# Issuing a two-stream decoder layer in the order of its Python code, with the Strassen sums one half product earlier

## The chip, the core and the metric

The kernel runs on one core of a Trainium2 chip. A core has a matrix engine (TensorE, PE), a vector engine (VectorE, DVE), a scalar engine (ScalarE, ACT), GpSimd (POOL) and SyncE (SP), which here only sends DMA transfers. Each engine works off its own queue of instructions; semaphores make one engine wait for another. The metric is the device time of the whole kernel in microseconds (us).

## What is computed

One decoder layer on 256 tokens of width 2048 in float32: ten projections of `x`, causal attention, a chunked spatial gate, cross-attention into 256 memory tokens, three branch projections, merging by sigmoid gates, an output projection and a layer norm.

```python
proj = x @ w_in
q_a, k_a, v_a, z_a, u_g, v_g, z_g, q_c, z_c, g_logit = split(proj)
y_a = moba_attention(q_a, k_a, v_a) * silu(z_a)
y_g = spatial_gating(u_g, v_g, w_s, b_s, ln_v_g, ln_v_b) * silu(z_g)
y_c = memory_attention(q_c, mem @ w_mem_k, mem @ w_mem_v) * silu(z_c)
gates = sigmoid(g_logit)
merged = (gates[0] * (y_a @ w_branch_attn) + gates[1] * (y_g @ w_branch_sgu)
          + gates[2] * (y_c @ w_branch_mem))
x = layer_norm(DN_ALPHA * x + merged @ w_out)
```

## The kernel before

All products are made from split operands: `split` (L57 to L60) makes a rounded `hi` on ScalarE and the remainder `lo` on VectorE, and TensorE sums hi x hi, hi x lo and lo x hi. So each weight tile goes from a DMA through ScalarE and VectorE before TensorE can use it.

Two streams share the engines. The classic stream (`classic`) makes, in this order, the tiles of `zc`, `qc` with the memory attention, three tiles of `za`, the branch projection 2 (`gated_branch(2, 0)`), the rest of `za`, `q` and `k` with the causal attention, three tiles of `ug`, `gated_branch(0, 1)`, the rest of `ug`, the gating tiles `zg`, and `gated_branch(1, 2)`: 160 steps of half a weight chunk each. A chunk is 1 MB in a `raw` tile; `c_half` keeps two halves split ahead of the one in use, with three slots each for `hi` and `lo`. The Strassen stream (`s_stream`) makes eight blocks of 1024 columns (gate logits, `v`) by seven products of half blocks each: 112 steps. `s_prep(s + 2)`, called behind the matmuls of step s, makes the sum of weight blocks that a product needs (L311), splits it into `sh` and `sl` (four slots in all) and asks for the next block (`s_load`) once the old one has been read. The loop at the end of `classic` sets how the streams take turns: after classic step c it runs Strassen steps until their number has reached 112(c - 2)/144.

What a step leaves to do for others (evacuating accumulators, stores) is put on a list, `late`, and called behind the matmuls of the next step (`step`). Stages of the attention heads are called one by one by `tick`, at the end of each tile.

`gated_branch` (L697) takes each of four column blocks n with two accumulators, one for each half of the tokens, out of three slots `acc`. At the start of a block it loads the gate logits `sg` (L703) and takes their sigmoid (L704, ScalarE). After its four halves `gated` is put on `late`: it multiplies accumulator and gate (L726, VectorE), adds the sum so far `mp`, loaded at L725 (L728), and stores it, or in the last branch calls `merged` at once, in which TensorE transposes the result and the engines split it into `mhl`. Then come the output projection and `normalise`.

The order in which instructions stand in the queues is not that of the code: the context is opened with `schedule_with_timeline_sim=True`, so a planner with its own model of time orders them, by data dependences, free slots and priority. Three kinds of transfers are held in order by `tc.issue_after`. Before the streams start, `mem_values` and `mem_keys` project the memory tokens, while `x_stages` splits `x` and makes the four sums `F` that the Strassen products need (`sum_parts`, stores `xw` to `xf`). `s_load` of block B11 uses the two slots of `F`.

Of the kernel before, what the change touches and what calls it, by code (L numbers as in the profile page):

```python
# [11 lines left out]
ALU = mybir.AluOpType  # L12
# [15 lines left out]
def decoder_layer(ctx, tc, xT, memT, x_tok, w_st, w_mv, w_mk, w_zc, w_qc, w_za, w_qk, w_ug, w_zg,  # L28
                  w_br, w_o, w_sT, sgu_bc, ln_g, ln_b, out):
    nc = tc.nc  # L30

    const = ctx.enter_context(tc.tile_pool(name="const", bufs=1))
    big = ctx.enter_context(tc.tile_pool(name="big", bufs=1))
# [17 lines left out]
    def new_sps(name):  # L51
        return psum.tile([P, 512], F32, tag="sps", name=name, bufs=3)
# [5 lines left out]
    def split(hi, lo, v):  # L58
        nc.scalar.activation(hi, v, AF.Copy)  # L59
        nc.vector.tensor_tensor(lo, v, hi.bitcast(F32), op=ALU.subtract)  # L60
# [26 lines left out]
    ptr = {"load": 0, "half": 0}  # L87
    hold = {}

    loaded = {}  # L90
    riders = {}

    def load_chunk(i):

        if 0 < i < 16:
            with tc.issue_after(loaded[i - 1].ins):
                load_one(i)
        else:
            load_one(i)
        for fn in riders.pop(i, ()):  # L100
            with tc.issue_after(loaded[i].ins):
                fn()

    def load_one(i):
        if i % 3 == 2 and i < 16 or i >= OUT and (i - OUT) % 3 == 2:
            t = big.tile([P, 2, 1024], F32, tag="vg", name=f"raw{i}")
        else:
            t = wts.tile([P, 2, 1024], F32, tag="raw", name=f"raw{i}", bufs=2)
        raw[i] = t
        if i < 8:  # L110
            a = w2(f"mraw{i}", (P, 2, S))
            act_raw[i] = a
            if i == 0:

                for kk in range(2):
                    nc.sync.dma_start(a[:, kk], memT[:, kk])
                    for c in (slice(0, 512), slice(512, 1024)):
                        loaded[i] = nc.sync.dma_start(t[:, kk, c], chunks[i][:, kk, c])
                return
            nc.sync.dma_start(a, memT[:, 2 * i:2 * i + 2, :])  # L120
        for h in range(2) if i < 4 else (slice(0, 2),):
            loaded[i] = nc.sync.dma_start(t[:, h], chunks[i][:, h])
# [5 lines left out]
    def load_after(c):  # L128
        while ptr["load"] < len(chunks) and room_after(ptr["load"]) <= c:
            ptr["load"] += 1  # L130
            load_chunk(ptr["load"] - 1)
# [153 lines left out]
    UNITS = 8  # L285
    PRODUCTS = ("M1", "M5", "M6", "M3", "M7", "M4", "M2")
    FORM = {"M5": 1, "M6": 2, "M3": 4, "M7": 3}
    rt, shl, xsf, sp = {}, {}, {}, {}

    def s_load(u, blk, h):  # L290
        if u >= UNITS:
            return
        tag, bufs = ("rA", 2) if blk == 0 else ("rB", 4)
        t = wts.tile([P, 2048], F32, tag=tag, name=f"b{blk}_{u}_{h}", bufs=bufs)
        nc.sync.dma_start(t, w_st[u, blk, h])
        rt[u, blk, h] = t

    B11, B12, B22, B21 = range(4)

    def s_prep(s):  # L300
        u, r = divmod(s, 14)
        if u >= UNITS:
            return
        p, h = divmod(r, 2)
        p = PRODUCTS[p]
        if p in FORM:
            t = wts.tile([P, 4, 2 * P], F32R, tag="xsf", name=f"xf{s}", bufs=3)
            nc.sync.dma_start(t.bitcast(F32), xf_d[FORM[p], h])
            xsf[s] = t
        b = lambda blk: rt[u, blk, h]  # L310
        sub = lambda o, x, y: nc.vector.tensor_tensor(o, x, y, op=ALU.subtract)  # L311
        src = {"M1": B11, "M5": B11, "M6": B11, "M4": B11, "M3": B22, "M7": B12, "M2": B21}[p]
        if p == "M5":
            sub(b(B11), b(B12), b(B11))
        elif p == "M6":
            sub(b(B11), b(B22), b(B11))
        elif p == "M4":
            sub(b(B11), b(B21), b(B11))
        hi = wts.tile([P, 2048], F32R, tag="shl", name=f"sh{s}", bufs=4)
        lo = wts.tile([P, 2048], F32R, tag="shl", name=f"sl{s}", bufs=4)  # L320
        split(hi, lo, b(src))
        shl[s] = (hi, lo)
        if p == "M3":
            sub(b(B12), b(B22), b(B12))
            s_load(u, B21, h)
        elif p == "M7":
            s_load(u + 1, B12, h)
        elif p == "M4":
            s_load(u + 1, B11, h)
        elif p == "M2":  # L330
            s_load(u + 1, B22, h)

    def snap(name):
        return work.tile([P, 512], F32, tag="snap", name=name, bufs=5)

    def s_stream(finish):

        bank, kept = {}, {}

        def keep(name, ps):  # L340
            kept[name] = snap(name)
            nc.scalar.activation(kept[name], ps, AF.Copy)

        def result(u, t, n, ps, name):
            r = kept[name]
            nc.vector.tensor_tensor(r, ps, r, op=ALU.add)
            finish(u, t, n, r)

        def evacuate(u, p):
            if p == "M1":  # L350
                keep(f"k1_{u}", bank["b"])
            elif p == "M5":
                keep(f"k5_{u}", bank["d"])
            elif p == "M6":
                keep(f"k6_{u}", bank["b"])
            elif p == "M3":
                result(u, 0, 1, bank["d"], f"k6_{u}")
            elif p == "M7":
                keep(f"k7_{u}", bank["b"])
                result(u, 1, 1, bank["b"], f"k5_{u}")  # L360
            elif p == "M4":
                result(u, 1, 0, bank["c"], f"k7_{u}")
            else:
                result(u, 0, 0, bank["a"], f"k1_{u}")

        BANK = {"M1": "b", "M6": "b", "M7": "b", "M5": "d", "M3": "d", "M4": "c", "M2": "a"}
        for s in range(14 * UNITS):
            u, r = divmod(s, 14)
            p, h = divmod(r, 2)
            p = PRODUCTS[p]  # L370
            if h == 0 and p in ("M1", "M5", "M4", "M2"):
                bank[BANK[p]] = new_sps(f"s{p}_{u}")
            ps = bank[BANK[p]]
            hi, lo = shl.pop(s)
            for kk in range(4):
                k = 4 * h + kk
                if p in FORM:
                    ah, al = xsf[s][:, kk, 0:P], xsf[s][:, kk, P:2 * P]
                else:
                    k += 0 if p == "M1" else 8  # L380
                    t = P if p == "M4" else 0
                    ah, al = xhl[:, k, t:t + P], xhl[:, k, S + t:S + t + P]
                c = slice(kk * 512, (kk + 1) * 512)
                first = h == 0 and kk == 0 and p in ("M1", "M5", "M4", "M2")
                last = h == 1 and kk == 3
                nc.tensor.matmul(ps, ah, hi[:, c], start=first, stop=False, skip_group_check=True)  # L386
                nc.tensor.matmul(ps, ah, lo[:, c], start=False, stop=False, skip_group_check=True)  # L387
                nc.tensor.matmul(ps, al, hi[:, c], start=False, stop=last, skip_group_check=True)  # L388
            xsf.pop(s, None)
            s_prep(s + 2)  # L390
            if h == 1:
                late.append(lambda u=u, p=p: evacuate(u, p))
            yield
# [45 lines left out]
    def mem_keys():  # L439
        for j in range(8):  # L440
            def fin(ps, j=j):
                v = w1(f"mk{j}")
                joined(v, ps, f"mk{j}")
                store(mk_d[j], v)
            yield from channel_tile(mem_k, f"mk{j}", fin)

    def run(gen):

        left = [True]

        def go():
            left[0] = next(gen, "end") != "end"
        while left[0]:
            step(go)
            yield
# [4 lines left out]
    for i, _ in enumerate(run(mem_keys())):  # L460
        if x_work:
            x_work.pop(0)()
        if i in (2, 4):
            with tc.issue_after(loaded[ptr["load"] - 1].ins):
                s_load(0, B12, i // 2 - 1)
        if i in (10, 12):
            for blk in (B11, B22):
                with tc.issue_after(loaded[ptr["load"] - 1].ins):
                    s_load(0, blk, i // 2 - 5)
    while x_work:  # L470
        x_work.pop(0)()
        step(lambda: None)
    s_prep(0)
    s_prep(1)


    yhl = {}
# [297 lines left out]
    C_STEPS, S_STEPS = 160, 14 * UNITS  # L775
    LEAD, TAIL = 2, 14
    cs, ss = classic(), s_stream(s_finish)
    done_c = done_s = 0
    for _ in run(cs):
# [136 lines left out]
```

## Time and profile before

| | us |
|---|---|
| median of 3 runs | 1010.97 (1009.83 to 1012.68) |
| the profiled execution | 1014.38 |
| its span | 1012.7 |
| TensorE busy in it | 982.4 (97%) |
| VectorE busy in it | 820.6 (81%) |
| ScalarE busy in it | 590.6 (58%) |

The span goes from the first to the last instruction of the profile; the execution's own time is 1.7 us longer. A busy TensorE is not TensorE at its peak, since matmuls overlap; the step from the start of one to the start of the next is what it costs.

### The profile page before, as it was taken

The numbers are of one execution on the slowest core, as the hardware profiler recorded it, in microseconds if no ns is written. First come the engines' busy times: TensorE is split into PE (matmuls) and PEld (weight loads), VectorE is DVE, ScalarE is ACT, GpSimd is POOL, SyncE is SP. The second block draws the span as 40 slices with busy tenths as digits, with TensorE's granted clock in tenths as the row PEclk, the third lists the DMA queues.
The fourth block names the chain that finished last, engine by engine and source line by source line (L and its number), as shares of the span: only waits on it lengthen the run. The fifth ranks groups of instructions, "written<-read, shape, count | busy, mean of one in ns | idle before, by whom it ended". The sixth has DMA issues, their size and how long they took to land.

```text
span 1012.7 us, 12913 instructions
## 1 busy us (share of the span) xinstructions
PE 982.4 (97%) x4888; PEld 826.9 (82%) x4888; DVE 820.6 (81%) x800; ACT 590.6 (58%) x646; POOL 12.0 (1%) x17
## 2 busy tenths in 40 slices
PE   9999899999999999999999999979998999999995
PEld 7788788888888788888888888858877888878885
DVE  5865987898779799888979898899979877676657
ACT  5654665565577566556556566867555559554430
POOL 0000000000000000000000000000000010000000
PEclk9999999999999999999999999989999999999998
DMA  8899589738965897598379648937994785778622
GB/s 330 313 387 414 181 304 348 277 132 296 364 223 168 295 382 278 165 362 346 134 271 356 236 139 281 382 106 269 414 366 147 284 286 183 249 259 303 238 84 83
DMA packets 68126, 269.28 MB, mean 266 GB/s; under 512 B 7521, under 2 KB 21601, under 8 KB 45537
## 3 DMA queue, kind: packets, MB, share of 16 engines
q1 hardware_dynamic: 68064, 268.47, 72.2%
q8 instruction: 38, 0.62, 0.2%
q14 instruction: 24, 0.19, 0.0%
HBM read 245.37 MB, written 23.07 MB: 265 GB/s over the span
## 4 chain that ended last, share of the span: by engine, by line
PE 85%; DVE 5%; ACT 4%; DMA 3%; issue 2%; POOL 0%; SPq 0%; DVEq 0%; ACTq 0%
PE sM L386 9%; PE sM L387 9%; PE sM L388 9%; PE b L713 4%; PE b L714 3%; PE b L712 3%; PE zc L187 3%; PE k L187 3%; PE qc L187 3%; PE za L187 3%; PE q L187 3%; PE mk L187 3%; PE o L800 3%; PE o L799 3%; PE o L798 3%; PE mv L423 3%
## 5 line engine op out<-in xcount | busy, mean ns | idle before, releaser
L59 ACT ACTIVATE hi<-raw 128x1024 fp32r<-128x1024 f32 (+1 forms) x218 | 228.3, 1051 | 191.4 <-PE o L800 29.1
L60 DVE TENSOR_TENSOR lo<-raw,hi 128x1024 fp32r<-128x1024 f32 (+1 forms) x218 | 263.1, 1214 | 77.2 <-ACT hi L59 76.4
L60 DVE TENSOR_TENSOR sl<-b,sh 128x2048 fp32r<-128x2048 f32 x112 | 256.3, 2291 | 57.1 <-ACT sh L59 56.7
L59 ACT ACTIVATE sh<-b 128x2048 fp32r<-128x2048 f32 x112 | 214.4, 1915 | 99.6 <-PE sM L387 89.3
L311 DVE TENSOR_TENSOR b<-b,b 128x2048 f32<-128x2048 f32 x64 | 146.3, 2289 | 8.0 <-DMA b<-in_w_st_dram 7.8
L386 PE MATMUL sM<-sh,xf 128*128 128x512 f32 x256 | 101.3, 396 | 6.5 <-ACT sh L59 6.5
L387 PE MATMUL sM<-sl,xf 128*128 128x512 f32 x256 | 100.6, 393 | 2.5 <-DVE sl L60 2.5
L388 PE MATMUL sM<-sh,xf 128*128 128x512 f32 x256 | 100.2, 391 | 0.0
L387 PE MATMUL sM<-sl,xhl 128*128 128x512 f32 x192 | 76.8, 400 | 0.6 <-DVE sl L60 0.6
L386 PE MATMUL sM<-sh,xhl 128*128 128x512 f32 x192 | 77.4, 403 | 0.0
L713 PE MATMUL b<-lo,yhl 128*128 128x512 f32 x192 | 76.1, 397 | 1.2 <-DVE lo L60 1.2
L388 PE MATMUL sM<-sh,xhl 128*128 128x512 f32 x192 | 76.3, 397 | 0.0
L714 PE MATMUL b<-hi,yhl 128*128 128x512 f32 x192 | 74.9, 394 | 0.0
L712 PE MATMUL b<-hi,yhl 128*128 128x512 f32 x192 | 74.0, 398 | 0.9 <-ACT hi L59 0.9
L386 PEld LDWEIGHTS sM<-sh,xf 128*128 128x128 f32 x256 | 48.3, 189 | 18.3 <-ACT sh L59 7.9
L387 PEld LDWEIGHTS sM<-sl,xf 128*128 128x128 f32 x256 | 48.2, 188 | 12.9 <-DVE sl L60 3.2
L388 PEld LDWEIGHTS sM<-sh,xf 128*128 128x128 f32 x256 | 48.1, 188 | 10.3
L187 PE MATMUL ug<-xhl,hi 128*128 128x512 f32 x128 | 46.3, 400 | 1.5 <-ACT hi L59 1.5
L187 PE MATMUL q<-xhl,hi 128*128 128x512 f32 x128 | 46.5, 399 | 0.0
L187 PE MATMUL qc<-xhl,hi 128*128 128x512 f32 x128 | 46.2, 400 | 0.0
L187 PE MATMUL zc<-xhl,hi 128*128 128x512 f32 x128 | 45.7, 398 | 0.4 <-ACT hi L59 0.4
L187 PE MATMUL k<-xhl,hi 128*128 128x512 f32 x128 | 46.0, 397 | 0.0
(296 smaller groups left out, 1853.1 us busy)
## 6 DMA issues: line engine op xcount, KB each, us to landing
b<-in_w_st_dram SPq DMA_DIRECT2D x64, 1024.0 KB, 7.2
xf<-xf SPq DMA_DIRECT2D x64, 512.0 KB, 6.0
raw<-in_w_br_dram SPq DMA_DIRECT2D x24, 1024.0 KB, 6.8
raw<-in_w_qk_dram SPq DMA_DIRECT2D x16, 1024.0 KB, 7.3
raw<-in_w_o_dram SPq DMA_DIRECT2D x16, 1024.0 KB, 5.4
raw<-in_w_mk_dram SPq DMA_DIRECT2D x8, 1024.0 KB, 10.1
raw<-in_w_zc_dram SPq DMA_DIRECT2D x8, 1024.0 KB, 6.5
raw<-in_w_qc_dram SPq DMA_DIRECT2D x8, 1024.0 KB, 7.6
```

What stands on the lines that cost most here:

```text
L59: nc.scalar.activation(hi, v, AF.Copy)
L60: nc.vector.tensor_tensor(lo, v, hi.bitcast(F32), op=ALU.subtract)
L187: nc.tensor.matmul(ps, hi, x, start=first, stop=False)
L311: sub = lambda o, x, y: nc.vector.tensor_tensor(o, x, y, op=ALU.subtract)
L386: nc.tensor.matmul(ps, ah, hi[:, c], start=first, stop=False, skip_group_check=True)
L387: nc.tensor.matmul(ps, ah, lo[:, c], start=False, stop=False, skip_group_check=True)
L388: nc.tensor.matmul(ps, al, hi[:, c], start=False, stop=last, skip_group_check=True)
L423: nc.tensor.matmul(ps[t][n], lhs, rhs[:, n * 512:(n + 1) * 512], start=(k == 0 and rhs is hi and lhs is xh[t]), stop=(k == KT - 1 and lhs ...
L712: nc.tensor.matmul(ps[t], yh, hi[:, c], start=(k == 0), stop=False)
L713: nc.tensor.matmul(ps[t], yh, lo[:, c], start=False, stop=False)
L714: nc.tensor.matmul(ps[t], yl, hi[:, c], start=False, stop=(k == 7))
L798: nc.tensor.matmul(ps[:, 0:n], mh, hi, start=first, stop=False)
```

## The change

The context is put under a manual schedule: on every engine and on the DMA queue the instructions now stand in the order in which the Python code emits them. The `issue_after` blocks become plain calls. The sum of weight blocks is taken out of `s_prep` into `s_sum`, which is called with s + 3 just ahead of `s_prep(s + 2)`: it is emitted one half product ahead of the split that reads it. The subtraction for M3 stays behind its split.

```diff
+    ctx.enter_context(tc.manual_schedule())
...
         if 0 < i < 16:
-            with tc.issue_after(loaded[i - 1].ins):
+            if True:
                 load_one(i)
...
         for fn in riders.pop(i, ()):
-            with tc.issue_after(loaded[i].ins):
+            if True:
                 fn()
...
+    def s_sum(s):
+
+        u, r = divmod(s, 14)
+        if u >= UNITS:
+            return
+        p, h = divmod(r, 2)
+        other = {"M5": B12, "M6": B22, "M4": B21}.get(PRODUCTS[p])
+        if other is not None:
+            o = rt[u, B11, h]
+            nc.vector.tensor_tensor(o, rt[u, other, h], o, op=ALU.subtract)
+
...
-        if p == "M5":
-            sub(b(B11), b(B12), b(B11))
-        elif p == "M6":
-            sub(b(B11), b(B22), b(B11))
-        elif p == "M4":
-            sub(b(B11), b(B21), b(B11))
...
             xsf.pop(s, None)
+            s_sum(s + 3)
             s_prep(s + 2)
...
         if i in (2, 4):
-            with tc.issue_after(loaded[ptr["load"] - 1].ins):
+            if True:
                 s_load(0, B12, i // 2 - 1)
...
     s_prep(0)
     s_prep(1)
+    s_sum(2)
```

## Rows read from the trace of the kernel before

**Rows 1.** The page, busy us (share of the span) by engine, with instructions.

```profile
PE 982.4 (97%) x4888; PEld 826.9 (82%) x4888; DVE 820.6 (81%) x800; ACT 590.6 (58%) x646; POOL 12.0 (1%) x17
```

**Rows 2.** Waits of TensorE: waiter, what for, us in total, times, longest.

```profile
PE sM L386 <- ACT sh L59: 6.5, 3, 2.8
...
PE zc L187 <- ACT hi L59: 0.4, 1, 0.4
```

**Rows 3.** Timeline of TensorE: start, us, instruction, idle before and its releaser.

```profile
109.28 0.80 PE L386 MATMUL sM<-sh,xf 128*128 128x512 f32 x1 [2.84 <-ACT sh L59]
109.88 0.63 PE L387 MATMUL sM<-sl,xhl 128*128 128x512 f32 x1
110.31 0.63 PE L388 MATMUL sM<-sh,xhl 128*128 128x512 f32 x1
...
117.57 0.40 PE L187 MATMUL zc<-xhl,hi 128*128 128x512 f32 x1
117.80 0.28 PE L188 MATMUL zc<-xhl,lo 128*128 128x256 f32 x1
117.92 0.40 PE L187 MATMUL zc<-xhl,hi 128*128 128x512 f32 x1
...
679.19 0.79 PE L386 MATMUL sM<-sh,xf 128*128 128x512 f32 x1 [1.31 <-ACT sh L59]
```

**Rows 4.** Groups of VectorE by line and shape: busy us, mean ns, idle before.

```profile
L60 DVE TENSOR_TENSOR lo<-raw,hi 128x1024 fp32r<-128x1024 f32 x214 | 260.3, 1224 | 74.8 <-ACT hi L59 74.0
L60 DVE TENSOR_TENSOR sl<-b,sh 128x2048 fp32r<-128x2048 f32 x112 | 256.3, 2291 | 57.1 <-ACT sh L59 56.7
L311 DVE TENSOR_TENSOR b<-b,b 128x2048 f32<-128x2048 f32 x64 | 146.3, 2289 | 8.0 <-DMA b<-in_w_st_dram 7.8
...
L726 DVE TENSOR_TENSOR sg<-b,sg 128x512 f32<-128x512 f32 x24 | 15.6, 684 | 0.0
...
L663 DVE TENSOR_TENSOR vg<-vg,sc 128x256 f32<-128x256 f32 x16 | 6.4, 423 | 0.0
```

**Rows 5.** Groups of ScalarE by line and shape, the same columns.

```profile
L59 ACT ACTIVATE hi<-raw 128x1024 fp32r<-128x1024 f32 x214 | 225.8, 1059 | 189.0 <-PE o L800 29.1 <-PE b L714 25.1 <-PE zc L187 15.1
L59 ACT ACTIVATE sh<-b 128x2048 fp32r<-128x2048 f32 x112 | 214.4, 1915 | 99.6 <-PE sM L387 89.3 <-DVE b L311 4.8 <-DVE sg L726 3.5
...
L704 ACT ACTIVATE sg<-sg 128x512 f32<-128x512 f32 x24 | 14.9, 628 | 13.2 <-DMA sg<-gl 13.0
L704 ACT ACT_TABLE_LOAD x9 | 11.5, 1283 | 4.5 <-DMA sg<-gl 3.2 <-issue 0.9
```

**Rows 6.** Timelines of TensorE, VectorE and ScalarE in the first branch.

```profile
322.58 0.39 PE L712 MATMUL b<-hi,yhl 128*128 128x512 f32 x1
...
323.48 0.39 PE L387 MATMUL sM<-sl,xf 128*128 128x512 f32 x1
...
326.32 1.29 DVE L726 TENSOR_TENSOR sg<-b,sg 128x512 f32<-128x512 f32 x2
...
335.99 1.29 ACT L704 ACTIVATE sg<-sg 128x512 f32<-128x512 f32 x2 [4.39 <-DMA sg<-gl]
```

**Rows 7.** The transfers of line L703 (`sg`): time from issue to landing.

```profile
DMA to landing us min/median/max: 2.5/3.7/7.8
```

**Rows 8.** DMA issues by line: times, KB each, median us to landing.

```profile
b<-in_w_st_dram SPq DMA_DIRECT2D x64, 1024.0 KB, 7.2
...
xf<-xw SPq DMA_DIRECT2D x8, 512.0 KB, 7.4
```

**Rows 9.** Matmuls of L386 from 786 to 858: us, PE busy (count), PEld busy, clock.

```profile
786.00:858.00 72.00, 12.26 (x31) 5.88 (x32) 1.00 0.71 253
```

**Rows 10.** Timeline of VectorE in the last normalisation.

```profile
1002.86 2.86 DVE L815 SCALAR_TENSOR_TENSOR xres<-xres,fmv,g_bc 128x512 f32<-128x512 f32 x5
```

**Rows 11.** One stretch: us, busy us of PE, PEld, DVE, ACT, POOL, then clock.

```profile
655.00:742.00 87.00, 81.80 (x346) 66.03 (x345) 79.44 (x71) 53.38 (x50) 0.00 (x0) 0.94 0.73 282
```

More of the change, by code (lines that the diff above doesn't have):

```diff
@@ L467, in decoder_layer @@
             for blk in (B11, B22):
-                with tc.issue_after(loaded[ptr["load"] - 1].ins):
+                if True:
                     s_load(0, blk, i // 2 - 5)
```

## The prediction

> **What bounds the kernel now.** The page's busy table comes first. The reader is to see TensorE at 97% and VectorE at 81% [rows 1]: TensorE sets the time, so the change can only bring what TensorE waits, and can cost whatever new waits it makes. Second, TensorE's own waits: six kinds of them, from 6.5 down to 0.4 us (the first and the last are shown [rows 2]), are waits for a split half (`hi`, `lo`, `sh`, `sl`) that came in an unlucky order, 13.6 us in all. Third, the timeline of TensorE behind such a wait: after 2.84 us without work the matmuls of 512 columns start 0.43 us apart, the lower of its two clock levels, where 0.23 is the step at the upper one [rows 3]. Three such stretches stand in the trace (6, 7 and 13 matmuls at 0.2 us extra each; the first and the last are shown), 5.4 us. So all that a perfect order could give back is 13.6 + 5.4 = 19 us; the start, the last reductions and the output lie outside both streams.
>
> **Base.** The profiled execution took 1014.4 us (span 1012.7 us), 3.4 us above the median of the runs. Sums are made on 1014.4; 3.4 comes off at the end.
>
> **What the edit does, part by part.** The `issue_after` blocks go; inside a strict order they say nothing, cost 0. `s_sum` moves a subtraction of 2.29 us [rows 4] ahead of the split that reads it by one half: it fills the 1.92 us in which ScalarE makes `sh` [rows 5], and `sl` behind it comes 0.4 us later. There are 64 before and after; cost 0, since that split is wanted two halves later (above 10 us). The strict order is the real change: each queue now runs the Python order, and a wait holds all that is behind it. In the even parts (the tiles of `zc`, `qc`, `za`, `q`, `k`, `ug`) this fits: `late` puts every evacuation one step after its matmuls, and splits are emitted two halves ahead. TensorE's steps are 2.79 us for a classic half (8 pairs of 0.35 [rows 3]) and 2.72 us for a Strassen half or a branch half (12 x 0.227); VectorE needs 1.22 for a classic half and 2.29 + 2.29 x 64/112 = 3.6 for a Strassen half [rows 4]. So there the 19 us come back: **-19**.
>
> **Gated branches, second accumulator.** `gated_branch` takes two accumulators per column block n from a ring of three. The fourth matmul of block n+1 (0.68 us into its first half) therefore needs the multiply L726 that frees an accumulator of block n, and that multiply is emitted one step late. Now the planner fills the gap: from 322.58 on it runs a few matmuls of the first token tile and eleven Strassen matmuls until the multiply has come at 326.32 [rows 6]. In strict order TensorE stands. Call T the start of block n+1's first half.
> Counting by the loop's rule (Strassen halves done after classic step c: 112(c-2)/144 rounded up), blocks start at steps 39, 43, 47, 51; 103, 107, 111, 115; 145, 149, 153, 157. The first of each branch needs no multiply. In four of the others (43, 47, 51, 115) a Strassen half ends just at T. Its slots come free at T, ScalarE makes the next `sh` (1.92), VectorE `sl` (2.29), and only then the multiply (0.69) [rows 4, 5]: T + 5.0. Stall 5.0 - 0.7 = 4.3, **4 x 4.3 = 17**.
> In the other five the step before is a classic one, so L726 is emitted behind the first half's own split. ScalarE has ahead of that split the two sigmoids of block n+1, whose operand is sent for at about T (behind the weight load that waits for the split before). With the median landing of 3.7 us [rows 7]: operands T + 3.75, two sigmoids of 0.63 T + 5.0, `hi` 1.06 T + 6.1, `lo` 1.22 T + 7.3, multiply T + 8.0 [rows 4, 5]. Stall 7.3. Four times (111, 149, 153, 157) 29. At 107 SyncE is held until about T + 3.3 by a Strassen load that waits for the reading of its slot, so 10.6. One table load, 1.3 [rows 5], in the last branch. **Together 41.** Lower end with the shortest landing, 2.5: 35; upper with 7.8: 62 [rows 7]. In the last branch `merged` puts TensorE's transposes right behind the adds; the last add ends at T + 10, as does the rest of the stalled half, so they cost only at the end of the stream, where nothing is between: an operand `mp` of the same size, 3.7, then an add, a multiply and an add: **5** (4 to 9).
> The Trainium skill, "DMA: Bandwidth & Descriptors", section "Anatomy of one DMA", gives about 2.0 us plus the bytes over 436 GB/s for one transfer, 2.6 us for 256 KB (an estimate from that fit, which is for another issuing path). The shortest landing agrees with it, the median of 3.7 does not [rows 7]. By the page's price the 41 would be some 35. The row decides, since a 1 MB weight load is in flight ahead of it each time.
>
> **First block of the middle branch** (step 103): SyncE held to T + 4.6, landing T + 8.3, table load and sigmoids T + 10.9, split T + 13.2, wanted at T + 10.9: **2** (0 to 6).
>
> **From memory keys to classic.** `s_load(0, B11, 1)` takes the slot of the second `F` tile, which the last `sum_parts` frees; that one waits for an earlier store (7.4 us [rows 8]). So it is sent for at the end of the memory keys and lands 7.2 us later [rows 8]; `sh` of half 1 stands ahead of the classic `hi` on ScalarE, and `sl` and the sum ahead of `lo` on VectorE: about 14.3 us after the keys' end, wanted at 5.6: **9** (2 to 12).
>
> **The gating tiles** (`zg`). Now only 31 of the first matmuls of Strassen steps lie there, some 8 halves [rows 9]; strictly it is 12.4. VectorE then has 16 x 1.22 + 12.4 x 2.29 + 8 sums of 2.29 + gating (L663, 6.4 [rows 4], and five groups of 8 x 0.42, as long as one of L663) + four evacuations of 0.69, 92 us beside some 82 of TensorE (16 x 2.79 + 12.4 x 2.72 and the mixes); the two halves of lead hold about 5: **5** (0 to 10). POOL's few masks keep their order, 0.
>
> **Ends.** At the start ScalarE takes the second `memhl` piece ahead of the first `hi`: 1. In the last normalisation the five L815 now stand behind the square root instead of beside it [rows 10]: 0.5. **1.5** (0.5 to 3).
>
> **Clock.** After 1.3 to 2.8 us of idling 6 to 13 matmuls ran on the lower level [rows 3], 1.2 to 2.6 us lost, 1.9 in the middle. Eleven stalls above 2.5 us: **21** (13 to 36).
>
> **Sum:** 17 + 41 + 5 + 2 + 9 + 5 + 1.5 + 21 = 101.5, less 19: +82.5, 1096.9; less 3.4: **1094 us**. With all lower ends (17 + 35 + 4 + 0 + 2 + 0 + 0.5 + 13 - 19 = 53) 1064, with all upper ones and only 13 given back (18 + 62 + 9 + 6 + 12 + 10 + 3 + 36 - 13 = 143) 1154.
>
> **Rivals.**
> (a) Short stalls. If the sigmoids' operands come in time (SyncE runs further ahead than I think), only the chains within engines are left: 4 x 4.3, and 5 x (1.06 + 1.22 + 0.69 - 0.68 = 2.3), 3 at the end, 4 elsewhere, 36 in all, and 5 for the clock: 36 + 5 - 19 = +22, less the 3.4 **1033 us**. For: the landing's minimum of 2.5 [rows 7]. Against: such operands already keep ScalarE waiting 4.39 us at 336 [rows 6].
> (b) Faster. The multiply is done before the fourth matmul asks: that needs L726 ahead of the split of the same step on VectorE, so that it ends by T + 0.7. It decides all nine stalls and their clock. Then 19 us come back and only 1.5 to 4 are paid: **995 us**. For: none of TensorE's waits now names L726. Against: it is emitted behind the split, and a strict queue can't put it ahead.
> (c) VectorE becomes the bound. Each chain that goes from VectorE to ScalarE and back (softmax, gated values) idles VectorE 0.5 to 1.5 us, some 24 times, in parts where it is as much as 91% busy (79.44 of 87 us [rows 11]): up to 30 us on top, **1124 us**, inside the forecast's upper half.
> (d) The order isn't strict, slots being given out by the planner: then little changes, **1008 to 1014**.
> The Trainium skill, "PSUM — Partial Sum Buffer", section "Engine vs sequencer instructions", says that the queues of ScalarE and VectorE are strictly first in, first out, and that matmuls start and end in program order. By that rule (b) would need another emission. The trace of before can't show it, its program order being the planner's.
>
> **How the numbers follow.** Forecast with (c): 0.66. (a) 0.16. (b) 0.13. (d) 0.03, of it 0.02 within the resolution. Beyond 1154: 0.02. About 0.3% is what a measurement of this kernel can tell from no change. The range leaves out (b), (d) and the top: 1018 to 1140; the likeliest case's own is 1064 to 1154. Faster 0.13, same 0.02, slower 0.85.
>
> **What the changed profile would show.** Right: TensorE waits for L726 nine times, 4 to 11 us each; ScalarE L704 waits on the load `sg`; the granted clock is below 1 in the slices of the three branches and 1 in the tiles between them; the stall of 660 to 680 is gone; VectorE's busy sum stays near 820. Wrong: no such waits (then (a) or (b)); a TensorE idle spread evenly over all stages (then (c)). The sum fails first in the landing of `sg` and in the clock's price, as they carry 62 of the 101.5 us.

## The result, and the profile after

The changed kernel takes 1169.1 us (1166.97 to 1172.03 in four runs) where the kernel before takes 1010.6: a ratio of 1.157, 95% interval 1.1535 to 1.1599. The forecast was 1094, in a range of 1018 to 1140: the direction and the place were right, the size was too small by 75 us. The measured time lies beyond even the sum of all the forecast's upper ends, 1154, to which it gave a chance of 0.02. The new lines stand eight lower in the code at the branches: L726 is now L734, L728 is L736, L703 is L711, L704 is L712, L712 to L714 are L720 to L722, L59 and L60 are L60 and L61.

The page of the changed kernel, busy us (share of the span) by engine, then the granted clock of TensorE in forty slices:

```profile
PE 1018.8 (87%) x4888; PEld 845.7 (72%) x4888; DVE 831.7 (71%) x800; ACT 568.8 (49%) x638; POOL 9.5 (1%) x17
...
PEclk9999999999988899999999997879899999778998
```

Against [rows 1] the span grew by 153.8 us (1166.5 less 1012.7). TensorE's busy time grew by 36.4 with the same 4888 instructions: that is, in the main, the lower clock. The other 117.4 are idle time. VectorE and ScalarE do about the work that they did before (831.7 us for 820.6, 568.8 for 590.6).

TensorE's waits in the changed kernel (waiter, releaser: us in total, times, longest), where [rows 2] began with 6.5 us:

```profile
PE b L720 <- DVE sg L734: 72.6, 9, 15.8
PE ug L189 <- DVE lo L61: 12.0, 3, 8.5
PE b L720 <- ACT hi L60: 7.5, 4, 3.3
PE zc L188 <- ACT hi L60: 6.9, 2, 6.2
PE mT L748 <- DVE sg L736: 6.3, 2, 6.1
PE b L721 <- DVE lo L61: 5.1, 7, 0.8
PE zg L189 <- DVE lo L61: 4.7, 3, 3.2
PE sM L392 <- DMA xf<-xf: 4.3, 6, 1.1
PE sM L393 <- DVE sl L61: 4.1, 3, 2.6
```

The first row is the forecast's row: nine waits for the multiply that frees an accumulator. Four of these nine, in the timeline of TensorE (start, us, instruction, idle before and its releaser): two behind a Strassen half, two behind a classic step, and behind one of them the step of the matmuls:

```profile
353.04 0.79 PE L720 MATMUL b<-hi,yhl 128*128 128x512 f32 x1 [4.11 <-DVE sg L734]
...
795.21 0.79 PE L720 MATMUL b<-hi,yhl 128*128 128x512 f32 x1 [4.02 <-DVE sg L734]
...
733.52 0.79 PE L720 MATMUL b<-hi,yhl 128*128 128x512 f32 x1 [15.85 <-DVE sg L734]
734.12 0.63 PE L721 MATMUL b<-lo,yhl 128*128 128x512 f32 x1
734.54 0.63 PE L722 MATMUL b<-hi,yhl 128*128 128x512 f32 x1
734.97 0.63 PE L720 MATMUL b<-hi,yhl 128*128 128x512 f32 x1
...
996.80 0.79 PE L720 MATMUL b<-hi,yhl 128*128 128x512 f32 x1 [9.59 <-DVE sg L734]
```

Why the longest is so long is read from the other three queues between 712 and 736 us. First the DMA queue, then ScalarE, then VectorE:

```profile
714.80 6.85 SPq L296 DMA_DIRECT2D b<-in_w_st_dram  x2
722.46 0.33 SPq L123 DMA_DIRECT2D raw<-in_w_br_dram  x1
722.84 0.97 SPq L711 DMA_DIRECT2D sg<-gl  x2
723.90 0.92 SPq L733 DMA_DIRECT2D mp<-mc  x2
...
716.54 0.63 ACT L761 ACTIVATE vg<-k 128x512 f32<-128x512 f32 x1 [3.25 <-DVE k L352]
...
729.40 1.27 ACT L712 ACTIVATE sg<-sg 128x512 f32<-128x512 f32 x2 [9.48 <-DMA sg<-gl]
730.57 1.04 ACT L60 ACTIVATE hi<-raw 128x1024 fp32r<-128x1024 f32 x1
...
719.01 2.29 DVE L61 TENSOR_TENSOR sl<-b,sh 128x2048 fp32r<-128x2048 f32 x1 [2.50 <-ACT sh L60]
...
731.64 1.23 DVE L61 TENSOR_TENSOR lo<-raw,hi 128x1024 fp32r<-128x1024 f32 x1 [9.21 <-ACT hi L60]
732.79 0.68 DVE L734 TENSOR_TENSOR sg<-b,sg 128x512 f32<-128x512 f32 x1
```

It reads as a chain. The block begins at 717.0 (733.52 less the 15.85 and three matmuls of 0.23). Before that ScalarE has stood 3.25 us at the evacuation `vg<-k`, and VectorE 2.50 us for the `sh` behind it, so that `sl`, the last reader of a Strassen block's slot, ends at 721.3. The DMA queue is held by two Strassen blocks until 721.7 and sends the gates `sg` at 722.84; they land at 729.4; ScalarE has stood 9.48 us at the sigmoid, with the split `hi` behind it; VectorE has stood 9.21 us at `lo`, with the ready multiply behind it; TensorE stands for the accumulator. Three engines wait for one 256 KB load that none of the waiting instructions but the sigmoid needs. Not all of the 15.85 us is the load's: in two runs below in which `sg` is not waited for, or hardly at this block, it still stalls 6.5 and 6.6 us by the chain that begins at `vg<-k`.

### The profile page after: what moved, and what is told of

Same layout as the page of the kernel before. It is cut to its first block, busy times and chain, and to the rows that moved or that the text cites. A ratio compares the mean times of both kernels' runs of the same rounds, so it can differ in the third digit from the quotient of the medians.

```text
span 1166.5 us, 12791 instructions
## 1 busy us (share of the span) xinstructions
PE 1018.8 (87%) x4888; PEld 845.7 (72%) x4888; DVE 831.7 (71%) x800; ACT 568.8 (49%) x638; POOL 9.5 (1%) x17
## 4 chain that ended last, share of the span: by engine, by line
PE 49%; DVE 18%; DMA 17%; issue 8%; ACT 7%; SPq 1%; ACTq 0%; DVEq 0%
DVE sl L61 6%; PE sM L392 5%; DMA sg<-gl 5%; PE sM L393 5%; DVE lo L61 5%; PE sM L394 5%; PE mv L430 3%; DMA xf<-xf 3%; PE o L807 3%; PE o L806 3%; ACT sh L60 3%; PE o L808 3%; ACT hi L60 3%; DVE b L310 2%; PE b L720 2%
## 5 line engine op out<-in xcount | busy, mean ns | idle before, releaser
L61 DVE TENSOR_TENSOR lo<-raw,hi 128x1024 fp32r<-128x1024 f32 (+1 forms) x218 | 262.6, 1212 | 179.8 <-ACT hi L60 178.4
L61 DVE TENSOR_TENSOR sl<-b,sh 128x2048 fp32r<-128x2048 f32 x112 | 256.4, 2289 | 64.3 <-ACT sh L60 60.4
L60 ACT ACTIVATE sh<-b 128x2048 fp32r<-128x2048 f32 x112 | 214.2, 1912 | 151.6 <-PE sM L393 145.1
L60 ACT ACTIVATE hi<-raw 128x1024 fp32r<-128x1024 f32 (+1 forms) x218 | 225.6, 1042 | 91.1 <-PE o L808 28.8
L720 PE MATMUL b<-hi,yhl 128*128 128x512 f32 x192 | 85.6, 446 | 80.2 <-DVE sg L734 72.6
L310 DVE TENSOR_TENSOR b<-b,b 128x2048 f32<-128x2048 f32 x48 | 109.6, 2284 | 0.0
L720 PEld LDWEIGHTS b<-hi,yhl 128*128 128x128 f32 x192 | 40.8, 213 | 94.7 <-DVE sg L734 76.4
L721 PE MATMUL b<-lo,yhl 128*128 128x512 f32 x192 | 83.6, 436 | 5.1 <-DVE lo L61 5.1
L722 PE MATMUL b<-hi,yhl 128*128 128x512 f32 x192 | 82.2, 428 | 0.0
L394 PEld LDWEIGHTS sM<-sh,xf 128*128 128x128 f32 x256 | 48.5, 189 | 11.1
L712 ACT ACTIVATE sg<-sg 128x512 f32<-128x512 f32 x24 | 15.0, 630 | 82.1 <-DMA sg<-gl 81.9
L721 PEld LDWEIGHTS b<-lo,yhl 128*128 128x128 f32 x192 | 41.1, 214 | 16.0 <-DVE lo L61 7.7
L188 PE MATMUL zg<-xhl,hi 128*128 128x512 f32 x128 | 48.9, 418 | 1.5 <-ACT hi L60 1.5
```

Source lines behind the costliest of these rows:

```text
L188: nc.tensor.matmul(ps, hi, x, start=first, stop=False)
L310: nc.vector.tensor_tensor(o, rt[u, other, h], o, op=ALU.subtract)
L720: nc.tensor.matmul(ps[t], yh, hi[:, c], start=(k == 0), stop=False)
L721: nc.tensor.matmul(ps[t], yh, lo[:, c], start=False, stop=False)
L722: nc.tensor.matmul(ps[t], yl, hi[:, c], start=False, stop=(k == 7))
```

## The experiments

The kernel before took 1011 to 1012 us beside each of these runs. The theories that the expectations name: A, a strict queue holds the multiply behind a split and behind the sigmoids' loads, and the clock falls after each stall. B, the order costs a little everywhere, VectorE being the bound. C, TensorE's own fixed order is the cause. D, the late landing of loads behind a held DMA queue is the cause by itself. E, the loss is a product of late loads and of queues that stand at them; F, the engines' fixed orders suffice without the loads.

**1. Which half of the change costs.** The sums moved, the planner's order kept:

```diff
-        if p == "M5":
-            sub(b(B11), b(B12), b(B11))
...
+            s_sum(s + 3)
             s_prep(s + 2)
```

> The planner's order of the kernel before, with only the sums of weight blocks issued one half product earlier (the other half of the change alone). Theory A: the sums have no part in the loss, 1011 us, within 3 us of the kernel before. Rival: the sums take VectorE's slots and the loss is partly theirs: 1020 us or more.

Measured: 1011.5 us, ratio 0.9998 (0.9988 to 1.0008). The moved sums cost and bring nothing; the whole loss is the order's.

**2. Which engine's order costs.** The same kernel with the strict order on some queues only:

```diff
-    ctx.enter_context(tc.manual_schedule())
+    ctx.enter_context(tc.manual_schedule(engines={...}))
```

> Strict order on the DMA queue alone. Theory A: the queue's order matters only where an engine is held at a load, 1011 to 1025 us. Rival D (the late landing of loads behind a held DMA queue is the cause by itself): 1050 us or more.

> Strict order on ScalarE and VectorE alone; TensorE and the DMA queue as the planner orders them. Theory A: these two queues carry most of it, 1040 to 1100 us. Theory C and rival D: 1025 us or less.

> Strict order on TensorE alone; the planner orders the other engines and the DMA queue. Theory A: the multiply and the splits can be put ahead of what waits, so the nine stalls are short: 1015 to 1035 us. Theory C: most of the loss is here, 1100 us or more.

> Strict order on ScalarE, VectorE, GpSimd and the DMA queue; TensorE's matmuls are ordered by the planner. Theory A (queues of ScalarE and VectorE hold what TensorE needs, so TensorE has little else to run in a stall): about half of the loss stays, 1060 us or more. Theory C (TensorE's own fixed order makes the loss, because it can no longer run the other stream's matmuls while one operand is late): 1030 us or less.

> Strict order on TensorE, ScalarE, VectorE and GpSimd; only the DMA queue as the planner orders it. Theory E (a product: the loads sg, mp and the weights are sent late by a strict DMA queue, and ScalarE and VectorE stand at them with all that is behind): most of the branches' loss goes, 1080 us or less, and the waits of ScalarE for sg fall from 82 us to under 20. Theory F (TensorE's, ScalarE's and VectorE's fixed orders suffice; the accumulators are late whatever the loads do): 1130 us or more.

| strict order on | us | over before |
|---|---|---|
| the DMA queue | 1032.5 | 21 |
| ScalarE and VectorE | 1059.0 | 48 |
| TensorE | 1046.1 | 35 |
| all but the DMA queue | 1100.4 | 88 |
| all but TensorE | 1146.5 | 135 |
| all | 1169.1 | 158 |

The intervals of the ratios are at most 0.6% to either side. One caution: these kernels have the change's plain calls in place of `issue_after`, so where the DMA queue isn't strict nothing holds the first loads in order. The stage ahead of `zc` loses 18 to 22 us in the four kernels of this study of which that holds (the second, third and fourth line, and one of experiment 3), and 8 to 12 in the others; some 10 us of these lines belong to it.

TensorE's own order adds 23 us to the rest (158 less 135). The DMA queue's adds 70 (158 less 88, and some 10 more by the caution), but by itself only 21: what the queues cost does not add up, one order's cost depends on the others'. The rows of the loads `sg` say how: who waited for them (us, times), and their time from issue to landing. First with all strict, then with the DMA queue alone, then with all but the DMA queue:

```profile
  ACT sg L712: 81.9, 14
...
DMA to landing us min/median/max: 5.0/6.0/9.6
```

```profile
  ACT sg L712: 14.7, 5
...
DMA to landing us min/median/max: 5.0/6.0/9.1
```

```profile
  ACT sg L712: 0.8, 2
...
DMA to landing us min/median/max: 2.5/4.8/8.9
```

A strict DMA queue makes the landing long whoever orders the rest. By itself that cost only 5 us of stage loss in the branches (worked out as in experiment 3), since ScalarE was given other work before the load; it costs much in a ScalarE that must stand at it. So D alone falls short (1032.5 is above A's 1025 and far below D's 1050), and E, which expected 1080 or less for the last kernel where F expected 1130, is nearer to its 1100, though its bound was missed too: the nine waits remain there, with 41.3 us instead of 72.6:

```profile
PE b L720 <- DVE sg L734: 41.3, 9, 8.1
```

C falls with the kernel in which the planner orders TensorE alone: the accumulator is no longer named in its waits, and the time is lost all the same, at the splits behind the sigmoids:

```profile
PE b L720 <- ACT hi L60: 44.8, 18, 7.6
PE sM L392 <- DMA xf<-xf: 26.8, 15, 4.1
```

TensorE strict alone came out above A's 1035 for another reason, a wait of its transposes in the causal attention (21.7 us in four). The planner, which fixes TensorE's order by its own model before the run, found little else to put there while the other engines stand; no run here lets TensorE choose as it goes.

**3. Which stages cost.** The strict order switched off for the three branches, and the reverse, at the classic steps where they begin and end:

```diff
+        if done_c in (38, 102, 144):
+            strict.close()
+        elif done_c in (55, 119):
+            strict.enter_context(tc.manual_schedule())
```

> Strict order everywhere except in the three gated branches (classic steps 38 to 54, 102 to 118, 144 to the end of the streams), which the planner orders. By the prediction's sum the parts outside the branches cost 9 + 5 + 1.5 and some clock and give back most of 19: 1008 to 1020 us. By the losses per stage of the changed kernel's trace (time of a stage less its matmuls at full clock, after less before) these parts cost about 45 us: 1050 us.

> Strict order only in the three gated branches; the planner orders the rest. By the prediction's sum 17 + 41 + 5 + 2 + about 18 of clock, less 5 given back: 1011 + 78 = about 1090 us. By the losses per stage of the changed kernel's trace the branches cost 105 us: 1116 us. If the loss needs a queue that is strict from the start on, under 1050 us.

Measured: 1041.3 us without the branches, 1125.4 with the branches alone; 29 and 113 over before, 142 of the 158 together. Both came out nearer to the losses by stage (1050 and 1116) than to the prediction's sum (1008 to 1020 and 1090), and strict branches alone suffice: their loss does not need a queue that is strict from the start. To see where, each stage's loss was worked out from the timelines of TensorE: the stage's length less its matmuls at the upper clock (0.227 us for 512 columns, in proportion for fewer, 0.061 for 128). Stages end where the next tile's first matmul starts, but branch 1 ends behind its own last matmul, so that the wait for its last add stands under the output, which ends with its last matmul; a few matmul records are missing, so a figure is good to about 2 us.

| loss, us | to `zc` | `zc`, `qc` | `za` (both) | branch 2 | `q`, `k` | `ug` (both) | branch 0 | `zg` | branch 1 | output |
|---|---|---|---|---|---|---|---|---|---|---|
| before | 9.3 | 11.4 | 5.5 | 1.6 | 8.2 | 7.4 | 12.6 | 5.6 | 2.6 | 2.1 |
| all strict | 12.2 | 23.3 | 4.3 | 35.6 | 13.7 | 17.4 | 47.3 | 15.1 | 39.2 | 11.1 |
| strict but in the branches | 10.6 | 25.1 | 4.6 | 4.3 | 12.6 | 8.1 | 7.9 | 13.4 | 1.5 | 2.4 |
| strict in the branches | 21.0 | 6.8 | 5.4 | 27.2 | 8.3 | 20.5 | 39.8 | 7.7 | 34.9 | 1.9 |

All strict, the branches lose 105 us more than before (122.1 less 16.8) and the rest 48. Strict in the branches alone they lose 85 more; the run's other 22 over before stand mainly ahead of `zc` (11.7), where nothing holds the first loads in order, and in `ug` (13.1), on both sides of a strict branch.

**4. What in the branches holds the multiply.** First, the multiply one step earlier:

```diff
                 if half == 3:
+                    for t in range(2):
+                        nc.vector.tensor_tensor(g[t], ps[t], g[t], op=ALU.mult)
                     late.append(lambda n=n, ps=ps, g=g: gated(b, order, n, ps, g))
```

> Strict order as in the changed kernel; only the multiply that frees an accumulator is issued right behind the fourth half of its block instead of one step later. Theory A (the loss sits where a strict queue holds that multiply behind a split and behind the sigmoids' loads, and the clock falls after each such stall): the nine waits for L734 (72.6 us) shrink to under 1 us each; in the five blocks that follow a classic step the weight half behind the sigmoids is still late by 3 to 5 us each, so some 20 us come back as waits for hi and lo; the clock gives back some 20: 1169 - 73 + 20 - 20 = about 1096 us. Theory B (strict order costs a little in every stage, VectorE being the bound): the time moves elsewhere and stays above 1140 us.

Measured 1153.3 us in one run: a miss by 57. The waits for the multiply did shrink, and were given back at the next instruction behind the same load; TensorE's waits in this kernel (waiter, releaser: us, times, longest):

```profile
PE mT L749 <- DVE sg L737: 27.0, 4, 7.5
PE b L720 <- ACT hi L60: 22.0, 7, 6.6
PE b L720 <- DVE sg L725: 15.8, 5, 5.4
```

Second, the gates early (`fetch` sends the two loads `sg`, `sigmoid` issues the sigmoids) and the multiply left where it was:

```diff
-                nc.sync.dma_start(g[t], gl_d[b, t, n])
-                nc.scalar.activation(g[t], g[t], AF.Sigmoid)
...
+                if half == 1:
+                    fetch(n + 1)
                 if half == 3:
+                    sigmoid(n + 1)
```

> Strict order; the multiply stays one step late, but the gate operands sg of the next block are sent for after the second half of a block and their sigmoids are issued at its end, so the landing of sg is taken away. Theory A with the landing as the mis-sized term: the five long waits for the multiply (56.3 us) fall to 2.3 us each (11.5), the four short ones (16.4 us) stay as they are; with 12 to 15 us of clock 1169 - 45 - 13 = about 1110 us. If not the landing but VectorE's own queue made them long, they stay at 7 us or more and the time is above 1130 us.

Measured 1138.0 us in one run. The waits for the multiply fell from 72.6 to 44.0: the four behind a Strassen half stayed (15.8), the five others fell from 56.3 to 28.1, not to 11.5:

```profile
PE b L731 <- DVE sg L748: 44.0, 9, 7.4
```

Third, both, with `mp` sent two halves ahead:

> Strict order; multiply right behind its block, gate operands and their sigmoids early, and the sum so far (mp) sent for two halves ahead. Theory A: no wait for L734 is left (72.6), the waits for hi in the branches (7.5), the one behind the add at 832 us (8.5) and the one at the end (6) go too, with some 27 us of clock: 1169 - 95 - 27 = about 1047 us; granted clock above 0.98. Theory B: above 1100 us.

Measured 1093.5 us, ratio 1.081 (1.078 to 1.084): the best strict version, 46 us above what was expected. What is left of the nine waits is 11.5 us in four. The longest, 5.42 us at 702.27, is a different chain, seen on ScalarE and VectorE:

```profile
695.73 0.63 ACT L778 ACTIVATE vg<-k 128x512 f32<-128x512 f32 x1 [3.25 <-DVE k L352]
...
695.01 0.68 DVE L352 TENSOR_TENSOR k<-sM,k 128x512 f32<-128x512 f32 x1
698.19 2.29 DVE L61 TENSOR_TENSOR sl<-b,sh 128x2048 fp32r<-128x2048 f32 x1 [2.50 <-ACT sh L60]
...
701.54 1.28 DVE L744 TENSOR_TENSOR sg<-b,sg 128x512 f32<-128x512 f32 x2
```

ScalarE stands at the evacuation `vg<-k` until VectorE, which is busy with splits, has added its part; then VectorE stands 2.50 us for the `sh` that was queued behind `vg<-k`; the multiply comes behind both. Work goes from one engine to the other and back, and each way is paid in full.

Fourth, only the place of the gates' loads in the DMA queue (`c_half` sends the weight load):

```diff
             for half in range(4):
+                if half == 3 and n < 3:
+                    fetch(n + 1)
                 hi, lo = c_half()
```

> Strict order as in the changed kernel; only the two loads sg of the next block are sent ahead of the last weight load of the block before instead of behind it. Theory A with the place in the queue as the mis-sized term: their median landing falls from 6.0 to about 3.7 us, the five long waits for the multiply (56 us) by about 3 us each, with the clock 1169 - 15 - 5 = about 1150 us. If the landing is long because the DMA engines are shared with every transfer in flight and not because of the place in the queue, the landing stays at about 6 us, and only the earlier sending helps: 1160 us or more.

Measured 1145.2 us, ratio 1.132 (1.129 to 1.134). The sum came out near the first theory's, its reason did not: the landing did not fall.

The loads `sg`, and the DMA queue ahead of one block:

```profile
DMA to landing us min/median/max: 5.1/5.9/7.9
```

```profile
709.23 6.86 SPq L296 DMA_DIRECT2D b<-in_w_st_dram  x2
716.13 0.90 SPq L711 DMA_DIRECT2D sg<-gl  x2
717.13 0.64 SPq L123 DMA_DIRECT2D raw<-in_w_br_dram  x1
717.87 0.91 SPq L742 DMA_DIRECT2D mp<-mc  x2
```

The five long waits fell from 56.3 to 37.0 because the loads were sent earlier. That they stand ahead of the weight load didn't shorten their landing; they still go out in one burst with two Strassen blocks, a weight chunk and `mp`. The edit took one 1 MB load from ahead of them and left others there: each of the 24 had a 1 MB load sent in the 3 us ahead of it. So this run doesn't show what a clear queue would bring.

**5. A version that beats both?** With TensorE alone strict, the stages from the second branch to the output lost 13 us less than before, while `q` and `k` with the attention heads lost 28 us more. So the kernel before was given a strict TensorE from a classic step on:

```diff
+        if done_c == 96:
+            pe.enter_context(tc.manual_schedule(engines={mybir.EngineType.PE}))
```

> The kernel before with TensorE alone in strict order from classic step 96 (the end of the causal attention) to the end of the streams; nothing else changed. The run with TensorE alone strict lost 20 us in its heads and at the start, but from step 96 to the end of the streams its loss by stage was 15 us against 28 us before. Theory A: that gain stays if the rest is left to the planner, 998 to 1004 us. Rival: the gain was only an effect of the stages before it being late, 1011 us or more.

> The kernel before with TensorE alone in strict order from classic step 102 (ahead of the second branch, behind the last attention heads) to the end of the streams. From step 96 on it gained 14 us of loss in the stages behind and lost 11 in the last attention heads. If these two are separate, 998 to 1004 us; if the gain only moves, 1009 to 1012 us.

Measured: 1010.7 us from step 96, ratio 0.9985 (0.9975 to 0.9994), and 1023.3 from step 102, ratio 1.0115. The gain moves with the border: behind step 96 the loss by stage fell by 14 us, and 11 came back in the last heads; from step 102 the stage of `q` and `k` kept its time, the tiles of `ug` behind it, into which the last heads reach, lost 15, and the branch gained nothing. Both missed what was expected, and the second is slower by 11 us. The first is 1.5 us ahead, under the 0.3% that this kernel's measurement can tell; no version beats the kernel before by an amount that matters.

## Why the prediction was right and wrong, step by step

Its rows were the right ones: nine waits for the multiply, on the steps that it named, ScalarE at the load `sg`, a lower clock in the branches, VectorE's busy time near 820 (831.7); two of the nine, 15.85 and 12.82, were longer than its 4 to 11 us. Each term beside TensorE's idle time in the changed kernel:

| term | forecast | measured |
|---|---|---|
| four blocks behind a Strassen half | 17 | 16.4 |
| five blocks behind a classic step | 41 | 56.3 |
| end of the streams | 5 | 6.3 |
| first block of the middle branch | 2 | 4.1 |
| memory keys to classic | 9 | 8.2 |
| `zg` | 5 | 7.0 |
| start, last normalisation | 1.5 | 1.7, at the start |
| `ug` | 0 | 12.0 |
| other waits for splits and loads in the streams | 0 | about 20 |
| waits given back | -13.6 | see below |
| clock, less 5.4 given back | 15.6 | 36.4 |

**The four short stalls, the transition and the end** were sized right: chains of durations from [rows 4, 5], each counted from a start that the queue's order fixes.

**The five long stalls.** The step "with the median landing of 3.7 us", and "whose operand is sent for at about T", are the terms that failed. The last branch shows the first alone: sent at 986.93, 0.4 us after T (986.5), landed at 992.64, 5.7 instead of 3.7 [rows 7]; 7.3 + 0.4 + 2.0 = 9.7, measured 9.59. Block 107: sent 2.5 us later than forecast (T + 5.9 for T + 3.3) and 6.6 to landing: 10.6 + 2.5 + 2.9 = 16.0, measured 15.85. Block 111: sent at T + 4.1 and 5.1 to landing: 7.3 + 4.1 + 1.4 = 12.8, measured 12.82. So the chain was right to 0.2 us; its input was a median over two kinds of loads. The trace of before shows both. Of its 24 loads `sg`, the twelve with a 1 MB load sent in the 3 us ahead of them landed in 3.7 to 7.8 us, median 7.0, and the other twelve in 2.5 to 4.6, median 2.9. One pair of each kind, the DMA queue and then the time to landing of the two `sg`:

```profile
298.89 0.33 SPq L122 DMA_DIRECT2D raw<-in_w_br_dram  x1
299.31 0.86 SPq L703 DMA_DIRECT2D sg<-gl  x2
DMA to landing us min/median/max: 7.4/7.5/7.6
...
333.15 0.94 SPq L703 DMA_DIRECT2D sg<-gl  x2
DMA to landing us min/median/max: 2.7/2.8/2.8
```

The forecast itself wrote that a 1 MB weight load is in flight ahead of `sg` each time, and so had the condition in hand, but took the median of all. With 7.0 the term is 41 + 5 x 3.3 = 57.5, close to the measured 56.3, though in part by luck: the five loads landed after 5.0 to 6.5 us, and two were sent late. In the changed kernel all 24 have such a load ahead. The experiments fit: the median landing is 6.0 us with all queues strict, with the DMA queue alone and with all but TensorE, and 4.4 to 4.8 in the three kernels of experiment 2 with the DMA queue free. That blocks 107 and 111 sent their loads late has another cause than the landing: the load ahead of `sg` in the DMA queue waited until VectorE had read a slot (`sl`, ended at 721.3, and `lo`, ended at 757.5), and ahead of each VectorE had stood 2.50 us for an `sh` queued behind `vg<-k`.

The Trainium skill, "DMA: Bandwidth & Descriptors", section "Anatomy of one DMA", by which the forecast put 2.6 us for 256 KB as an estimate, is near the landings of before with no 1 MB load just ahead (median 2.9 us) and doesn't agree with those in strict order, of which the shortest was 5.0 us. The measurement decides. The rule of the Trainium skill in "PSUM — Partial Sum Buffer", section "Engine vs sequencer instructions", that the queues of ScalarE and VectorE are first in, first out, does agree: the ready multiply ran at 732.79, behind a `lo` that had stood 9.21 us. Rival (b) fell by this.

**"So there the 19 us come back."** This step failed. Of the planner's waits [rows 2] those for `sh` (6.5 us) are gone; those for `sl` and for the branches' `lo` are not (4.1 us for 3.1, 5.1 for 1.2). And the even parts got others of their own, which the forecast put at nothing: all strict, the stages outside the branches lose 48 us more than before, and with strict order there alone the run was 29 us slower, where the forecast had the even parts, the transition, `zg` and the ends together at a small gain or loss. The reason that it gave, evacuations one step late and splits two halves ahead, holds for a queue that stands at nothing; it doesn't hold for one that stands at a load, as VectorE does below. The transition (8) and `zg` (7) were forecast; the largest that was not lies at the first tile of `ug` behind the middle branch, where the block's last step is carried out:

```profile
820.01 0.33 SPq L296 DMA_DIRECT2D b<-in_w_st_dram  x1
820.39 1.67 SPq L733 DMA_DIRECT2D mp<-mc  x2
...
829.53 0.69 DVE L736 TENSOR_TENSOR sg<-sg,mp 128x512 f32<-128x512 f32 x1 [8.95 <-DMA mp<-mc]
...
832.74 0.58 PE L189 MATMUL ug<-xhl,lo 128*128 128x256 f32 x1 [8.48 <-DVE lo L61]
```

The forecast had seen that an operand `mp` asked for at the end has nothing to cover it, and priced it once, at the end of the stream. The middle branch ends in the same way, and there the add holds `lo`.

**The clock.** The price per stall was about right, their number was not. Summed from the timeline of TensorE, the extra time of matmuls at the lower level after a stall came to 12.3 us for the seven stalls of 2.5 to 5 us and 15.2 for the eight longer ones, 1.75 and 1.9 each; the forecast took 1.9. It counted eleven; there were fifteen, 27.5 us for its 21. All other matmuls lost another 37.5, where the kernel before lost 31.0 in all: 5.4 of these were credited to the strict order, and instead of that 6.5 came on top. These sums are good to a few us. The upper end that the forecast gave this term, 36, doesn't follow from its own numbers: eleven stalls at 2.6 are 29. And the clock was not 1 between the branches: 0.96 from 873 to 966 us.

**The rivals.** (a) needed landed gates: the kernel with a free DMA queue shows two stalls of 2.33 us in the last branch, where it had 2.3, but also 6.51 and 8.14 in the middle branch, and takes 1100.4. (c) VectorE is at 71%, so it isn't the bound; but its mechanism, the way from VectorE to ScalarE and back, holds the multiply in the middle branch: it is what is left of blocks 107 and 111 where `sg` is landed or early (6.51 and 8.14 us with the DMA queue free, 6.63 and 7.38 with the gates early), and the third part of experiment 4 shows it. The forecast did not put it into the stalls. (d) fell.

Not settled: why the best strict version still loses so much. By stage it loses 36 us more than before outside the branches and 40 inside, in many waits of up to 5 us; no run took these apart.

## What to carry to other kernels

In a strict order a load is a promise to every instruction behind its first reader, on that engine and on each engine that waits for one of those: ask for a small late operand well ahead of the block that reads it, and put nothing urgent behind its reader. When an order changes, take the durations of engine instructions from the old trace as they are, but the time from issue to landing only from those of its loads that have the same traffic ahead of them as the new order will put there. Don't book as gain the waits that a new order removes until the new order's own waits in the same stages are counted.

## What the runs showed of the hardware that was not expected

The landing of a 256 KB load had a median of 3.7 us and a minimum of 2.5 in the planner's order, and 6.0 and 5.0 when the queue sent it in bursts behind a wait, with the bytes of all loads unchanged. What went with it in both was a 1 MB load sent just ahead: median 7.0 with one and 2.9 without in the kernel before, and all 24 with one in the changed kernel. Whether the one makes the other was not tested by itself. And a stall's price in clock hardly depended on its length: the matmuls behind the 15.85 us stall lost 1.7 us, those behind the 4.02 us stall 1.8. Removing length without removing stalls gave nothing back: with the gates early, TensorE waited about 34 us less than in the changed kernel, and its busy time was 1022.8 us against 1018.8.
